# Three transformer blocks on one core: score maps on paired half rows, heads one chunk apart, and a first norm whose scale comes from token rows

## The chip, the cores and the metric

The kernel runs on one core of one Trainium2 chip. The metric is the device time of one execution in microseconds, the median over the runs. TensorE multiplies a stationary operand (a weight load, PEld in the profile) by a moving one into PSUM; VectorE (DVE), ScalarE (ACT) and GpSimd (POOL) do the elementwise work; SP issues nearly all DMAs.

## What is computed

256 tokens of width 1024 go through a first block and two equal blocks of a second kind. The first block, cut to what matters:

```
h = rms_norm(x, norm_g); proj = h @ w_in          # 1024 x 6144
dq, dk, dv, dg, mq, mk, mv, mg, gates = split(proj)
# differential attention: 4 heads, each with two score maps of 64-wide q and k
s = causal(q[:, m] @ k[:, m].T / 8)  for m in 0, 1
w = softmax(s0) - lam * softmax(s1);  o_a = rms_norm(w @ v) * silu(dg)
# block attention: 8 heads of 64; with 256 tokens there is one block, so it is causal attention
o_b = softmax(causal(q @ k.T / 8)) @ v * silu(mg)
merged = sigmoid(g_a) * (o_a @ w_branch_diff) + sigmoid(g_b) * (o_b @ w_branch_moba)
x = x + merged @ w_out;  x = x + sigmoid(x @ w_ple_gate) * (p @ w_ple)
x = rms_norm(x, final_g)
```

Each later block (twice) normalizes, projects, runs 4 retention heads and 8 stick-breaking heads (`z = q k^T`, strictly causal, log terms summed from the right), merges them with gates, and adds a squared-relu MLP of width 4096. A last norm ends it.

## The kernel before

**Arithmetic.** Every product is made in three matmuls of a reduced 32-bit type. An operand is split into a high part (a copy by ScalarE, which rounds) and a low part (the difference, by VectorE); then high x high, high x low and low x high are added in PSUM. `hilo` (lines 126 to 128) does it for activations, `split` (282 to 287) for weights, `norm_hilo` (194 to 197) for x times the norm's gain. The norm's scale per token is not in that operand: it is applied when a projection is taken out of PSUM.

**Chunks.** The weights come as 189 chunks of 1 MB in one stream. `fetch` (276) loads a chunk into one of three `raw` buffers, `split` makes `wh` and `wl` (three buffers each). The loop at line 1018 does for each chunk i: split chunk i+2, fetch chunk i+5, the matmuls of chunk i with their evacuation (`ch.banks`), and then one step of each thread that was there before. A chunk for `chunk_t` (353) holds 8 k tiles by 256 columns and makes two transposed 128-column tiles; a pair of chunks for `chunk_n` (366) holds k tiles 0 to 3 and 4 to 7 of 512 columns and makes both token halves with tokens on partitions. PSUM has 8 banks: 5 `acc` for the chunks and 3 `aux` for everything else.

**Order.** The program's text gives each engine an order, and a planner that simulates the engines rearranges it by readiness. Instructions stamped with the same order token keep their order among themselves on their engine. All loads but that of the gains are issued by SP in the planned order; a load that needs a free buffer holds those behind it.

**The head.** 14 warm-up matmuls (line 416) run on constants. x comes transposed, in two loads of four k tiles; the gains come through ScalarE's queue (137). Chunk 0 is loaded in two pieces and split in four, one per k tile; chunk 1 in two pieces, split in two. Squares of the x tiles (205, 207) are summed over the k tiles; `norm_scale` (235) sums over partitions by matmuls (220, 223), and gives the scale both as a row for all partitions and as a column for each token half. It runs when the first chunk pair is done, ahead of its evacuation.

**The first block's heads.** `block1_branch` (554) makes q, k and v of a branch in six chunks, then two gate chunks follow for each branch; the order is branch 0, all four gate chunks, branch 1. q and k are scaled and turned by `qk1_turn` (440) into `m1`, two 64-wide halves on 128 partitions. `soft_head` (470) is a thread for one pair of maps. In one step it makes both score maps (131 to 133, operands of 64 rows, `M` in the profile), adds the causal mask by a matmul of the mask with an identity (`mask`, 463), takes the row maxima (487), the exps (488) and the scaling by the reciprocals (494 to 499); in the next step it transposes the weights (505); then it multiplies by v (517, 536). Heads 0 and 1 step one chunk ahead of heads 2 and 3.

**The stick-breaking heads.** `sb_head` (755) makes the scores, adds its mask in the same way (761), and takes abs, exp and ln on ScalarE; a step later come the sums (772, 773), a step later the product with v.

## Time and profile before

| | |
|---|---|
| Median of 3 runs | 1169.01 us (1168.88 to 1169.1) |
| Profiled execution | 1168.73 us |
| Its span, first to last instruction | 1167.0 us |
| Mean granted TensorE clock | 0.997 |
| TensorE busy | 1155.9 us, 99% |
| VectorE, ScalarE, GpSimd busy | 876.3, 707.4, 221.2 us |

A row of the profile names the line, the engine, the operation, out<-in by tile names, partitions x elements and the number of instructions; then busy time, the mean of one, and idle time before it with what ended it. A matmul's busy time reaches to its modelled end, so two matmuls in a row overlap in it; their rate is seen from start to start.

### The profile page before, as it was taken

The page shows a single profiled execution, that of the slowest core. Times are in us where ns is not written, and L with a number is a line of the kernel's source. Part 1 is how long each engine was busy: PE and PEld are TensorE (multiplying, and loading weights), DVE is VectorE, ACT ScalarE, POOL GpSimd, SP SyncE. Part 2 cuts the span into 40 slices and gives each one's busy share as a digit, 9 for nine tenths or more (in the row PEclk, how much of TensorE's full clock was granted, in tenths as well). Part 3 has the DMA queues.
Part 4 walks back from the last instruction along what each step waited for, and adds up shares of the span by engine and source line. Part 5 has one row for each costly group of instructions (what it writes and reads, how often), then busy time and mean ns, then how long its engine had stood idle before and what let it go on. Part 6 is the DMA issues. An engine that isn't in the chain of part 4 may idle for free.

```text
span 1167.0 us, 17530 instructions
## 1 busy us (share of the span) xinstructions
PE 1155.9 (99%) x6642; PEld 1013.0 (87%) x6642; DVE 876.3 (75%) x1433; ACT 707.4 (61%) x1275; POOL 221.2 (19%) x242
## 2 busy tenths in 40 slices
PE   8999999999999999999999999999999999999997
PEld 6888889998888888888888888888888888888887
DVE  7766867778997766678877778987776677967664
ACT  6657656566567776556744646556777555846442
POOL 1014104015641122211000002652112112000001
PEclk9999999999999999999999999999999999999999
DMA  8544435545555444546555556454444555555541
GB/s 312 182 144 145 145 117 181 182 180 196 193 181 179 145 164 163 183 165 220 190 181 185 199 183 213 173 196 178 145 168 157 181 183 196 184 184 211 180 180 37
DMA packets 32164, 206.58 MB, mean 177 GB/s; under 512 B 3920, under 2 KB 6224, under 8 KB 8144
## 3 DMA queue, kind: packets, MB, share of 16 engines
q1 hardware_dynamic: 31936, 205.44, 49.3%
q8 instruction: 52, 0.85, 0.3%
q14 instruction: 32, 0.26, 0.1%
q10 hardware_dynamic: 144, 0.03, 0.0%
HBM read 202.31 MB, written 1.05 MB: 174 GB/s over the span
## 4 chain that ended last, share of the span: by engine, by line
PE 94%; DVE 4%; ACT 1%; issue 1%; DMA 0%; POOLq 0%; POOL 0%; DVEq 0%
PE acc L300 41%; PE acc L303 21%; PE acc L343 20%; DVE wl L287 2%; PE aux L131 2%; PE aux L133 2%; PE aux L132 2%; PE acc L133 1%; PE acc L132 1%; PE acc L131 1%; DVE X L666 1%; PE aux L466 1%; PE aux L773 1%; DVE X L197 1%; PE acc L331 1%
## 5 line engine op out<-in xcount | busy, mean ns | idle before, releaser
L287 DVE TENSOR_TENSOR wl<-raw,wh 128x1024 fp32r<-128x1024 f32 (+1 forms) x380 | 462.8, 1249 | 135.1 <-ACT wh L286 130.4
L286 ACT ACTIVATE wh<-raw 128x1024 fp32r<-128x1024 f32 (+1 forms) x380 | 380.4, 1047 | 198.7 <-PE acc L300 109.0
L300 PE MATMUL acc<-X,wh 128*128 128x512 f32 x1472 | 383.1, 394 | 0.6 <-DVE X L666 0.4
L300 PEld LDWEIGHTS acc<-X,wh 128*128 128x128 f32 x1472 | 263.5, 189 | 47.9 <-issue 1.2
L303 PE MATMUL acc<-X,wl 128*128 128x256 f32 x1472 | 221.5, 283 | 0.0
L303 PEld LDWEIGHTS acc<-X,wl 128*128 128x128 f32 x1472 | 206.8, 190 | 13.6
L320 ACT ACTIVATE f<-acc 128x256 f32<-128x256 f32 x216 | 79.4, 374 | 61.8 <-PE acc L303 61.6
L343 PE MATMUL acc<-wh,X 128*128 128x512 f32 x432 | 111.8, 392 | 0.5 <-DVE f L321 0.5
L321 DVE TENSOR_TENSOR f<-f,acc 128x256 f32<-128x256 f32 x216 | 87.7, 414 | 24.0 <-ACT f L320 22.1
L343 PEld LDWEIGHTS acc<-wh,X 128*128 128x128 f32 x432 | 80.0, 188 | 16.6 <-DVE f L321 0.7
L207 POOL TENSOR_TENSOR sq<-sq,f 128x256 f32<-128x256 f32 x30 | 31.5, 1051 | 274.7 <-ACT f L205 274.3
L666 DVE TENSOR_TENSOR X<-X,acc 128x256 f32<-128x256 f32 x112 | 45.8, 416 | 34.2 <-PE acc L303 33.6
L597 POOL TENSOR_TENSOR sig<-f,nr 128x256 f32<-128x256 f32 x48 | 40.9, 859 | 147.1 <-DVE f L321 122.0
L300 PE MATMUL acc<-A,wh 128*128 128x512 f32 x256 | 64.5, 393 | 0.0
L300 PE MATMUL acc<-B,wh 128*128 128x512 f32 x256 | 64.4, 392 | 0.0
L343 PE MATMUL acc<-wl,X 128*128 128x512 f32 x216 | 60.0, 393 | 0.0
L300 PEld LDWEIGHTS acc<-B,wh 128*128 128x128 f32 x256 | 46.1, 189 | 8.2
L300 PE MATMUL acc<-M,wh 128*128 128x512 f32 x192 | 53.0, 394 | 0.0
L300 PEld LDWEIGHTS acc<-A,wh 128*128 128x128 f32 x256 | 46.0, 189 | 8.1
L343 PEld LDWEIGHTS acc<-wl,X 128*128 128x128 f32 x216 | 40.0, 188 | 7.8
L300 PEld LDWEIGHTS acc<-M,wh 128*128 128x128 f32 x192 | 35.0, 188 | 6.9
L303 PEld LDWEIGHTS acc<-A,wl 128*128 128x128 f32 x256 | 35.1, 190 | 2.5
(224 smaller groups left out, 1687.0 us busy)
## 6 DMA issues: line engine op xcount, KB each, us to landing
raw<-in_wstream_dram SPq DMA_DIRECT2D x187, 1024.0 KB, 4.8
raw<-in_wstream_dram SPq DMA_DIRECT2D x4, 512.0 KB, 7.8
sig<-f SPq DMA_DIRECT2D x32, 64.0 KB, 4.6
B<-in_tables_dram SPq DMA_DIRECT2D x2, 768.0 KB, 6.0
X<-in_xt_dram SPq DMA_DIRECT2D x2, 512.0 KB, 6.3
out_dram<-M SPq DMA_DIRECT2D x4, 256.0 KB, 2.2
M<-in_g_final_dram SPq DMA_DIRECT2D x1, 512.0 KB, 4.5
cst<-in_tables_dram SPq DMA_DIRECT2D x1, 352.0 KB, 10.2
```

Of the source, the lines that this page charges most:

```text
L131: T.matmul(o, lhsT=lh, rhs=rh, start=start, stop=False, skip_group_check=True)
L132: T.matmul(o, lhsT=lh, rhs=rl, start=False, stop=False, skip_group_check=True)
L133: T.matmul(o, lhsT=ll, rhs=rh, start=False, stop=stop, skip_group_check=True)
L286: A.activation(ch.wh[:, k], ch.raw[:, k], AF.Copy)
L287: V.tensor_sub(ch.wl[:, k], ch.raw[:, k], f32(ch.wh[:, k]))
L300: T.matmul(ps, lhsT=ch.wh[:, k, w], rhs=x.rearrange("p c t -> p (c t)"), start=i == 0, stop=False, skip_group_check=True)
L303: T.matmul(ps[:, 0:S], lhsT=ch.wl[:, k, w], rhs=x[:, 0], start=False, stop=i == len(ks) - 1, skip_group_check=True)
L320: A.activation(t, ps[:, S:2 * S], AF.Copy)
L321: V.tensor_add(t, t, ps[:, 0:S])
L343: T.matmul(p[:, 0:w], lhsT=xs[:, k, t], rhs=ws[:, i, o], start=n == 0 and k == 0, stop=n == 2 and k == KT - 1, skip_group_check=True)
L597: G.tensor_mul(store[(c, i)][0][:, k % 2], fold(ps), st.n.rb)
L666: V.tensor_add(X[:, k], X[:, k], ps[:, o:o + S])
```

## The change

* **Head, k tile by k tile.** The gains lie in front of x in one tensor and come with its first tile. The loads of x and of chunk 0 alternate (one tile, one piece, one tile, one piece, two tiles, ...). Chunk 1 is split in four too, and multiplied in the order of chunk 0 (`mm_k`: by k tile, both token halves). Order tokens make ScalarE and VectorE take x tile, weight tile, x tile, and so on. Nine warm-up matmuls instead of 14.
* **First norm.** x comes once more with tokens on partitions (`xn`, 1 MB, issued behind chunk 2). ScalarE squares each row half with a sum; the scale per token is a column at once (`head_r`, at high priority). The row for all partitions, which the transposed gates need, is made three chunks later by four matmuls of ones with a scaled identity (`head_rows`).
* **Maps.** The 12 matmuls of a head alternate between the two maps, that is, between partitions 0 to 63 and 64 to 127; one map is in an `aux` bank, the other in an `acc` bank. An order token strings them together with the last matmul of each of the first 20 chunks. The mask is added by VectorE while it takes the maximum (one instruction, which writes the negated sum to SBUF); the exp then works in place. Scaling by the reciprocals is done by ScalarE.
* **Heads one chunk apart**, with one more chunk between the exps and the transposes, and for the differential heads between the sub-norm and its transpose; four buffers for exps instead of two. The gate chunks of a branch follow that branch. Both maps of a block-attention head are multiplied by v together (512 and 256 moving columns).
* **Stick-breaking heads.** The mask is added by VectorE. The buffers `ph` and `pl` hold two sets each, two of them instead of four single ones, for retention and norms too.

The diff, cut to its core (`mm` stands for `T.matmul` in the chunk loops):

```diff
-WARM = 14
+WARM = 9
+GW = 64
+PB = 2
...
+LAST1 = 20
...
+    def mm(*args, **kw):
+        last[0] = T.matmul(*args, **kw)
...
-    gc = tl([56], "gc")
-    nc.scalar.dma_start(out=gc, in_=a["gains"])
+    xg = tl([GW + KT * S], "X")
+    gc, X = xg[:, 0:GW], xg[:, GW:].rearrange("p (k t) -> p k t", k=KT)
+
+    def load_x(k0, k1):
+        sl = slice(GW + k0 * S if k0 else 0, GW + k1 * S)
+        load(xg[:, sl], a["xt"][:, sl])
...
-    msk = tl([384], "sig", bufs=4)
+    msk = tl([384], "msk")
+    tri_f = tl([P], "sig", bufs=4)
...
-    idr = tl([P], "idr", F32R)
-    mqr = tl([P], "mqr", F32R)
-    msr = tl([P], "msr", F32R)
+    m_seg = msk[:, P:2 * P], msk[:, 0:2 * P]
+    m_sb = msk[:, None, 2 * P:3 * P].to_broadcast([P, 2, P])
...
-    def new_norm(g, sub=None):
...
     def fetch(ch, n=1):
+
         ch.raw = shaped(ch, tl([2048], "raw", bufs=3))
         src = shaped(ch, a["wstream"][chunks.index(ch)])
         for k in pieces(ch, n):
             load(ch.raw[:, k], src[:, k])
+            yield
 
     def split(ch, n=2):
+
         ch.wh = shaped(ch, tl([2048], "wh", F32R, bufs=3))
         ch.wl = shaped(ch, tl([2048], "wl", F32R, bufs=3))
         for k in pieces(ch, n):
-            A.activation(ch.wh[:, k], ch.raw[:, k], AF.Copy)
-            V.tensor_sub(ch.wl[:, k], ch.raw[:, k], f32(ch.wh[:, k]))
+            h = A.activation(ch.wh[:, k], ch.raw[:, k], AF.Copy)
+            l = V.tensor_sub(ch.wl[:, k], ch.raw[:, k], f32(ch.wh[:, k]))
+            yield h, l
...
+            if ch is chunks[1]:
+                mm_k(ch, ps, x(), 4)
             for h in range(2):
-                mm_n(ch, ps[h], x(), 4, h)
+                if ch is not chunks[1]:
+                    mm_n(ch, ps[h], x(), 4, h)
                 run_pre()
                 evac(ps[h] if parts > 1 else ps[h][0], h)
...
-    X = tl([KT, S], "X")
-    n0 = new_norm(g_norm)
+    n0 = new_norm(g_norm, sq=False)
+    xn = tl([2, D], "M2")
     st.n = n0
     x_ = lambda: st.n.x
 
...
-    def head_hilo(i):
-        for k in range(4 * i, 4 * i + 4):
-            norm_hilo(n0, X[:, k], k)
...
-    def head_squares():
-        for k in range(KT):
-            norm_square(n0, X, k)
...
-    e_slot = [scr[:, i * 768:(i + 1) * 768].rearrange("p (m q) -> p m q", m=2) for i in range(2)]
-    o_slot = [scr[:, 1536 + i * 256:1536 + (i + 1) * 256].rearrange("p (h e) -> p h e", h=2) for i in range(2)]
-
-    def start1():
-        norm_scale(n0)
-        rq = tl([2], "rq")
-        V.tensor_scalar_mul(rq, n0.r[:, S:S + 4:2], 0.125)
-        n0.rq = [rq[:, h:h + 1] for h in range(2)]
-
-    pre.append(start1)
+    e_slot = [scr[:, i * 768:(i + 1) * 768].rearrange("p (m q) -> p m q", m=2) for i in range(4)]
+    o_slot = [scr[:, 3072 + i * 256:3072 + (i + 1) * 256].rearrange("p (h e) -> p h e", h=2) for i in range(2)]
+
+    def head_r():
+
+        ss, r, rq = tl([2], "hss"), tl([2], "hr"), tl([2], "rq")
+        for h in range(2):
+            A.activation(xn[:, h], xn[:, h], AF.Square, accum_out=ss[:, h:h + 1])
+        V.tensor_scalar(ss, ss, 1.0 / D, EPS, ALU.mult, ALU.add)
+        rsqrt(r, ss)
+        V.tensor_scalar_mul(rq, r, 0.125)
+        n0.rc, n0.rq = ([t[:, h:h + 1] for h in range(2)] for t in (r, rq))
+
+    def head_rows():
+
+        for _ in range(3):
+            yield
+        ps = aux()[:, 0:S]
+        for h in range(2):
+            dh, dl = tl([P], "ph", F32R, PB), tl([P], "pl", F32R, PB)
+            A.activation(dh, ident, AF.Copy, scale=n0.rc[h])
+            V.scalar_tensor_tensor(dl, ident, n0.rc[h], f32(dh), ALU.mult, ALU.subtract)
+            for d in (dh, dl):
+                T.matmul(ps[:, h * P:(h + 1) * P], lhsT=one_r, rhs=d, start=h == 0 and d is dh, stop=d is dl,
+                         skip_group_check=True)
+        n0.rb = tl([W], "nr")[:, 0:S]
+        V.tensor_copy(n0.rb, ps)
+        yield
+
+    threads.append(head_rows())
...
-    m1 = Pair("M2")
...
-    def mask(ps, m):
-
-        o = ps.rearrange("p (b s) -> p b s", b=2)[:, :, 0:P]
-        T.matmul(o, lhsT=idr, rhs=m[:, None, :].to_broadcast([P, 2, P]), start=False, stop=True, skip_group_check=True)
...
-        ps = [aux(), aux()]
-        for m in range(2):
-            r = slice(m * 64, m * 64 + 64)
-            for o, q0, kn in ((0, 0, 128), (128, 128, 256)):
-                q, k = slice(q0, q0 + 128), slice(0, kn)
-                mm3(ps[m][:, o:o + kn], qh[r, q], ql[r, q], kh[r, k], kl[r, k], o == 0, False)
-            mask(ps[m], mqr)
-        e = e_slot[idx % 2]
+        ps = [aux(), acc()]
+        for o, q0, kn in ((0, 0, 128), (128, 128, 256)):
+            for n, (q_, k_) in enumerate(((qh, kh), (qh, kl), (ql, kh))):
+                for m in range(2):
+                    r = slice(m * 64, m * 64 + 64)
+                    mm = T.matmul(ps[m][:, o:o + kn], lhsT=q_[r, q0:q0 + 128], rhs=k_[r, 0:kn],
+                                  start=o == 0 and n == 0, stop=n == 2, skip_group_check=True)
+                    tc.stamp_issue_order_token(mm.ins, "maps")
+        e = e_slot[idx % 4]
...
-                V.tensor_reduce(mx[:, i:i + 1], ps[m][:, lo:hi], AX.X, ALU.max, negate=True)
-                act(e[:, m, lo:hi], ps[m][:, lo:hi], AF.Exp, bias=mx[:, i:i + 1], accum_out=sm[:, i:i + 1])
+                em = e[:, m, lo:hi]
+                V.tensor_tensor_reduce(em, ps[m][:, lo:hi], m_seg[h], -1.0, 3e38, ALU.add, ALU.min, mx[:, i:i + 1])
+                act(em, em, AF.Exp, scale=-1.0, bias=mx[:, i:i + 1], accum_out=sm[:, i:i + 1])
...
-                V.tensor_scalar_mul(e[:, 1, lo:hi], e[:, 1, lo:hi], rs[:, 2 + h:3 + h])
+                A.activation(e[:, 1, lo:hi], e[:, 1, lo:hi], AF.Copy, scale=rs[:, 2 + h:3 + h])
                 V.scalar_tensor_tensor(e[:, 0, lo:hi], e[:, 0, lo:hi], rs[:, h:h + 1], e[:, 1, lo:hi], ALU.mult, ALU.add)
         else:
             for m in range(2):
                 for h, lo, hi in segs:
-                    V.tensor_scalar_mul(e[:, m, lo:hi], e[:, m, lo:hi], rs[:, 2 * m + h:2 * m + h + 1])
-        yield
-        wt = []
+                    A.activation(e[:, m, lo:hi], e[:, m, lo:hi], AF.Copy, scale=rs[:, 2 * m + h:2 * m + h + 1])
+        yield
+        yield
+        wh, wl = tl([2, 384], "ph", F32R, 2), tl([2, 384], "pl", F32R, 2)
         for m in range(1 if diff else 2):
             pt = aux()
             for o, _, _ in BLK:
                 T.transpose(pt[:, o:o + P], e[:, m, o:o + P], ident)
-            h, l = tl([384], "ph", F32R, 4), tl([384], "pl", F32R, 4)
-            hilo(h, l, pt[:, 0:384])
-            wt.append((h, l))
+            hilo(wh[:, m], wl[:, m], pt[:, 0:384])
         yield
...
             yield
+            yield
             pt = aux()[:, 0:S]
             for h in range(2):
                 T.transpose(pt[:, h * P:(h + 1) * P], o[:, h], ident)
             V.scalar_tensor_tensor(f, pt, subg, g1[:, idx], ALU.mult, ALU.mult)
...
-            for m in range(2):
-                h, l = wt[m]
-                vc = slice(j * P, (j + 1) * P)
-                mm3(po[:, m], vh[:, 0, vc], vl[:, 0, vc], h[:, 0:256], l[:, 0:256], m == 0, False)
-                mm3(po[:, m, 128:256], vh[:, 1, vc], vl[:, 1, vc], h[:, 256:384], l[:, 256:384], False, True)
+            vc = slice(j * P, (j + 1) * P)
+            mm3(po, vh[:, 0, vc], vl[:, 0, vc], wh[:, :, 0:256], wl[:, :, 0:256], True, False)
+            mm3(po[:, :, 128:256], vh[:, 1, vc], vl[:, 1, vc], wh[:, :, 256:384], wl[:, :, 256:384], False, True)
...
-                        threads.append(soft_head(4 * br + j, j, v, br == 0, 1 + j // 2))
+                        threads.append(soft_head(4 * br + j, j, v, br == 0, 1 + j))
...
-    block1_branch(0)
-    for c, b in enumerate((6, 7, 14, 15)):
-        gate1(c, b)
-    block1_branch(1)
+    for br, gates in ((0, (6, 7)), (1, (14, 15))):
+        block1_branch(br)
+        for c, b in enumerate(gates):
+            gate1(2 * br + c, b)
...
-        dh, dl = tl([384], "ph", F32R, 4), tl([384], "pl", F32R, 4)
+        dh, dl = tl([384], "ph", F32R, 2), tl([384], "pl", F32R, 2)
...
-        mm3(z[:, 256:384], kh[:, j, 128:256], kl[:, j, 128:256], qh[:, j, 128:256], ql[:, j, 128:256], False, False)
-        mask(z, msr)
+        mm3(z[:, 256:384], kh[:, j, 128:256], kl[:, j, 128:256], qh[:, j, 128:256], ql[:, j, 128:256], False, True)
+        zd = z.rearrange("p (b s) -> p b s", b=2)[:, :, 0:P]
+        V.tensor_add(zd, zd, m_sb)
...
-        h_, l_ = tl([384], "ph", F32R, 4), tl([384], "pl", F32R, 4)
+        h2, l2 = tl([2, 384], "ph", F32R, 2), tl([2, 384], "pl", F32R, 2)
+        h_, l_ = h2[:, 0], l2[:, 0]
         hilo(h_, l_, t)
...
-        h_, l_ = tl([384], "ph", F32R, 4), tl([384], "pl", F32R, 4)
+        h_, l_ = h2[:, 1], l2[:, 1]
         hilo(h_, l_, t)
...
+    def in_order(pair):
+        for ins, tok in zip(pair, ("head_act", "head_dve")):
+            tc.stamp_issue_order_token(ins.ins, tok)
...
     warm_up(WARM)
-    load_x(0)
-    fetch(chunks[0], 2)
-    load_x(1)
-    fetch(chunks[1], 2)
-    fetch(chunks[2])
-    head_hilo(0)
-    split(chunks[0], 4)
-    head_hilo(1)
-    split(chunks[1])
-    fetch(chunks[3])
-    head_squares()
+    f = fetch(chunks[0], 4)
+    load_x(0, 1)
+    next(f)
+    load_x(1, 2)
+    next(f)
+    load_x(2, 4)
+    drain(f)
+    load_x(4, 6)
+    f = fetch(chunks[1], 2)
+    next(f)
+    load_x(6, KT)
+    drain(f)
+    drain(fetch(chunks[2]))
+    load(xn, a["xn"])
+    for i in range(2):
+        f = split(chunks[i], 4)
+        for k in range(4 * i, 4 * i + 4):
+            in_order(norm_hilo(n0, X[:, k], k))
+            in_order(next(f))
+        drain(f)
+    drain(fetch(chunks[3]))
+    with tc.high_priority():
+        head_r()
+    m1 = Pair("M2")
     late_consts()
-    fetch(chunks[4])
+    drain(fetch(chunks[4]))
     for i, ch in enumerate(chunks):
         if i + 2 < n:
-            split(chunks[i + 2])
+            drain(split(chunks[i + 2]))
         if i + 5 < n:
-            fetch(chunks[i + 5])
+            drain(fetch(chunks[i + 5]))
         ready = list(threads)
         ch.banks(ch)
+        if i < LAST1:
+            tc.stamp_issue_order_token(last[0].ins, "maps")
         if i == 0:
             use_consts()
         for g in ready:
```

More of the change, by code (lines that the diff above doesn't have):

```diff
@@ L33 @@
 C_SB = 704
-C_MQ = 704
-C_MS = 832
-C_TRI = 960
-C_DEC = 1088
+C_Z = 704
+C_MQ = 832
+C_MS = 960
+C_TRI = 1088
+C_DEC = 1216
 C_ALL = C_DEC + 4 * 384
 NCHUNK = 189
+LAST1 = 20
 def _tables():
@@ L128, in hilo @@
         V.tensor_sub(lo, src, f32(hi))
+    last = [None]
+    def mm(*args, **kw):
+        last[0] = T.matmul(*args, **kw)
     def mm3(o, lh, ll, rh, rl, start, stop):
@@ L170, in use_consts @@
         V.tensor_scalar_mul(subg, subg, 1.0 - LAM_INIT)
-        V.tensor_copy(idr, ident)
-        V.tensor_copy(mqr, msk[:, 0:128])
-        V.tensor_copy(msr, msk[:, 128:256])
-        V.tensor_copy(tri, msk[:, 256:384])
+        V.tensor_copy(tri, tri_f)
         V.tensor_scalar_mul(neg1, ones, -1.0)
@@ L184, in tile_blocks, with new_norm @@
         pass
-    def new_norm(g, sub=None):
+    def new_norm(g, sub=None, sq=True):
         n = Norm()
@@ L189, in new_norm @@
         n.x = Pair("X2")
-        n.sq = tl([S], "sq")
+        n.sq = tl([S], "sq") if sq else None
         n.sq2 = tl([S], "M2") if sub is not None else None
@@ L194, in norm_hilo @@
     def norm_hilo(n, x, k):
-        A.activation(n.x.h[:, k], x, AF.Copy, scale=n.g[:, k:k + 1])
-        V.scalar_tensor_tensor(n.x.l[:, k], x, n.g[:, k:k + 1], f32(n.x.h[:, k]), ALU.mult, ALU.subtract)
+        h = A.activation(n.x.h[:, k], x, AF.Copy, scale=n.g[:, k:k + 1])
+        l = V.scalar_tensor_tensor(n.x.l[:, k], x, n.g[:, k:k + 1], f32(n.x.h[:, k]), ALU.mult, ALU.subtract)
+        return h, l
     def norm_square(n, X, k):
@@ L330, in mm_k @@
                 for n, (xs, ws) in enumerate(((x.h, ch.wh), (x.h, ch.wl), (x.l, ch.wh))):
-                    T.matmul(ps[h][0], lhsT=xs[:, k, t], rhs=ws[:, i], start=n == 0 and k == 0,
-                             stop=n == 2 and k == KT - 1, skip_group_check=True)
+                    mm(ps[h][0], lhsT=xs[:, k, t], rhs=ws[:, i], start=n == 0 and k == 0,
+                       stop=n == 2 and k == KT - 1, skip_group_check=True)
     def mm_n(ch, ps, x, k0, h):
@@ L342, in mm_n @@
                     k = k0 + i
-                    T.matmul(p[:, 0:w], lhsT=xs[:, k, t], rhs=ws[:, i, o], start=n == 0 and k == 0,
-                             stop=n == 2 and k == KT - 1, skip_group_check=True)
+                    mm(p[:, 0:w], lhsT=xs[:, k, t], rhs=ws[:, i, o], start=n == 0 and k == 0,
+                       stop=n == 2 and k == KT - 1, skip_group_check=True)
     pre = []
```

27 lines of the change are left out of this document (14 added, 13 removed).

## Prediction

> **What bounds the kernel now.** I read the page first: the share of each engine and the chain that ended last.
>
> ```profile
> span 1167.0 us, 17530 instructions
> PE 1155.9 (99%) x6642; PEld 1013.0 (87%) x6642; DVE 876.3 (75%) x1433; ACT 707.4 (61%) x1275; POOL 221.2 (19%) x242
> PE 94%; DVE 4%; ACT 1%; issue 1%; DMA 0%; POOLq 0%; POOL 0%; DVEq 0%
> ```
>
> TensorE is busy for 99% of the span and carries 94% of the chain. So a nanosecond taken out of its instruction stream is a nanosecond off the end, as long as the other engines keep up, and work moved to other engines costs nothing until one of them is late. Next I asked for the waits of PE, which tell where it stands still.
>
> ```profile
> PE acc L331 <- ACT wh L286: 2.2, 1, 2.2
> PE aux L416 <- DVE one_r L152: 1.3, 1, 1.3
> PE acc L343 <- DVE f L321: 0.5, 1, 0.5
> ```
>
> Only the start has a wait worth naming; nothing can be won from stalls later on. The busy time of a matmul is modelled to its end, so cost is read from start to start. The chain of waits, asked for a stretch of the last stage, gives the unit:
>
> ```profile
> 1028.38 21.79 PE acc L343 x96
> 1050.16 1.81 PE acc L300 x8
> 1051.98 0.95 PE acc L303 x8
> ```
>
> A matmul with 512 moving columns takes 21.79 / 96 = 0.227 us of the stream, one with 256 columns 0.95 / 8 = 0.119. Last, the busy time by stretch where the first block's heads run, since the change gives work there to other engines (us, then busy time and instructions of each engine):
>
> ```profile
> 42.00:82.00 40.00, 40.00 (x229) 33.07 (x228) 28.51 (x55) 22.89 (x49) 2.99 (x4) 1.00 0.40 137
> 82.00:120.00 38.00, 37.50 (x193) 31.39 (x192) 26.17 (x55) 29.11 (x71) 13.47 (x16) 1.00 0.40 143
> 120.00:170.00 50.00, 49.95 (x320) 43.55 (x319) 36.63 (x78) 32.11 (x73) 5.89 (x8) 1.00 0.34 125
> ```
>
> In these 128 us VectorE (third number) works 91.3 us, ScalarE (fourth) 84.1: 71% and 66%.
>
> **Part 1, the head.** The timeline of the first 17 us:
>
> ```profile
> 1.30 5.55 PE L416 MATMUL aux<-one_r 128*128 128x512 f32 x14 [1.30 <-DVE one_r L152]
> 5.56 0.42 ACT L205 ACTIVATE sq<-X 128x256 f32<-128x256 f32 x1 [3.12 <-DMA X<-in_xt_dram]
> 6.50 1.69 ACT L196 ACTIVATE X<-X,gc 128x256 fp32r<-128x256 f32 x4
> 7.02 2.62 DVE L197 SCALAR_TENSOR_TENSOR X<-X,gc,X 128x256 fp32r<-128x256 f32 x4 [1.06 <-ACT X L196]
> 8.40 2.17 ACT L286 ACTIVATE wh<-raw 128x512 fp32r<-128x512 f32 x4
> 9.07 1.11 PE L331 MATMUL acc<-wh,X 128*128 128x512 f32 x2 [2.22 <-ACT wh L286]
> 9.57 2.49 DVE L287 TENSOR_TENSOR wl<-raw,wh 128x512 fp32r<-128x512 f32 x4
> 11.75 1.27 PE L331 MATMUL acc<-wh,X 128*128 128x512 f32 x3
> 16.30 0.39 PE L331 MATMUL acc<-wh,X 128*128 128x512 f32 x1
> ```
>
> The matmul at 16.30 is the 24th and last of chunk 0. At 0.227 us each the 23 before it would need 5.2 us, so the stream stands as if it had run densely from 16.30 - 5.2 = 11.1 us. The real start is at 9.07: the first weight split waits behind squares and all four x tiles on ScalarE, the next matmuls wait for VectorE, and three of them run about 0.42 us apart (1.27 / 3), half speed, after a pause of 2.2 us.
>
> With the change one k tile of x (with the gains, 160 KB) and one of the weights (256 KB) come first, and the order on both engines is x tile, weight tile, x tile. The traffic of today's first 10 us, in slices of 0.25 us, and its transfers:
>
> ```profile
> GB/s 0 0 0 0 0 0 49 115 267 204 258 135 174 240 242 176 226 275 236 285 234 229 295 246 311 377 442 361 459 410 410 459 377 442 410 410 459 393 410 377
> X<-in_xt_dram SPq DMA_DIRECT2D x2, 512.0 KB, 6.3
> gc<-in_gains_dram ACTq DMA_DIRECT2D x1, 28.0 KB, 5.0
> ```
>
> Bytes flow from 1.6 us, at some 220 GB/s until 6 us and 410 after. 416 KB take 1.9 us at 220, so they are there no earlier than 3.5 us, and no later than the 5.5 us at which today's 512 KB of x release ScalarE; I take the middle, 4.5. Then come one x tile (1.69 / 4 = 0.42) and one weight tile (2.17 / 4 = 0.54) on ScalarE: the first matmul at about 5.5, just behind nine warm-up matmuls (1.30 + 9 x 5.55 / 14 = 4.9). Per k tile VectorE then needs 2.62 / 4 + 2.49 / 4 = 1.28 us and PE 6 x 0.227 = 1.36, so PE sets the pace. I add 0.8 us for about four first matmuls at half clock: dense from 6.3, 11.1 - 6.3 = **4.8 us** gained. Bounds: 6.1 (dense from 5.0) and 2.0 (x as late as today, 7.0, six slow matmuls, 0.8 us of late tiles: dense from 9.1). Supply behind it: through chunk 2 and the 1 MB of token rows 5.3 million bytes are to be moved, at 410 GB/s by about 15 us, chunk 3 2.6 us later, and chunk 3 is due at 6.3 + 3 x 5.45 = 22.6. The token rows pass SP's queue ahead of chunk 3; the wait of chunk 3 for a free raw buffer ends earlier too, because chunk 0 is split earlier. The norm's sums on PE (six short matmuls) go and four matmuls for the row of scales come: taken as nothing, covered by no wait.
>
> **Part 2, the score maps.** PE's timeline of the second map of head 0, with the mask of the first before it:
>
> ```profile
> 51.58 0.39 PE L466 MATMUL aux<-mqr,idr 128*128 128x256 f32 x1
> 51.89 0.32 PE L131 MATMUL aux<-M 64*128 64x128 f32 x1
> 52.06 0.27 PE L132 MATMUL aux<-M 64*128 64x128 f32 x1
> 52.16 0.27 PE L133 MATMUL aux<-M 64*128 64x128 f32 x1
> 52.28 0.33 PE L131 MATMUL aux<-M 64*128 64x256 f32 x1
> 52.45 0.28 PE L132 MATMUL aux<-M 64*128 64x256 f32 x1
> 52.56 0.27 PE L133 MATMUL aux<-M 64*128 64x256 f32 x1
> 52.77 0.39 PE L466 MATMUL aux<-mqr,idr 128*128 128x256 f32 x1
> 52.99 0.86 PE L300 MATMUL acc<-X,wh 128*128 128x512 f32 x3
> ```
>
> Six half-row matmuls take 52.77 - 51.89 = 0.88 us, a mask 0.31 when half rows follow (51.58 to 51.89) and 0.22 otherwise: turning from 128 to 64 rows costs 0.09, and back also (52.56 to 52.77 is 0.21, the one before 0.11). A head is 2 x 0.88 + 0.31 + 0.22 = 2.29 us. In the new form there are 12 half-row matmuls with no mask and one turn back, 0.09. No row shows two half-row matmuls on different row halves side by side, so I bound them. Without any overlap each takes what one of its kind takes in a run, 0.11 to 0.12 (52.06 to 52.16, 52.45 to 52.56): 12 x 0.115 + 0.09 = 1.47, 0.82 saved. With full overlap two cost what one does, 0.057 each: 0.78, 1.51 saved. If every alternation cost the turn of 0.09: 2.55, 0.26 lost. The matmul rows lean to neither of the first two, so I take their middle, 0.086 each: 1.12, 1.17 saved, for 8 heads **9.3 us** (bounds -2.1 and 12.1).
> The Trainium skill, "TensorE: Matmul & The Clock Gate", part 3 on packing small matmuls, says that matmuls on different row groups run at once, a few ns apart; by it the part is 12.1 instead of 9.3. No row here tests that. Its page "TensorEngine Tiling (Array Packing)", key properties, says a switch of tiling mode drains the array; the 0.31 against 0.22 above agrees, and it would put no such price on alternating row halves.
>
> **Part 3, the other masks.** In the later layers' 16 stick-breaking heads:
>
> ```profile
> 363.13 0.33 PE L466 MATMUL aux<-msr,idr 128*128 128x256 f32 x1
> 363.30 0.28 PE L131 MATMUL aux<-M 128*128 128x256 f32 x1
> ```
>
> 0.17 each, **2.7 us** saved. In its place VectorE adds 128x256 from PSUM, 0.41 us by the same shape at line 321, in front of the head's ScalarE chain. What hides it is the next chunk's 32 matmuls (5.5 us) between a head's scores and the sums that use them; gone, it costs 16 x 0.41 = 6.6.
>
> **Part 4, weights times values of the block-attention heads.** One map of one head now:
>
> ```profile
> 159.29 0.33 PE L131 MATMUL aux<-ph,vh 128*128 128x256 f32 x1
> ...
> 159.70 0.22 PE L131 MATMUL aux<-ph,vh 128*128 128x128 f32 x1
> ...
> 159.98 0.52 PE L505 MATMUL aux<-cst,B 128*128 128x128 f32 x3
> ```
>
> 0.69 us, 1.38 for both. Joined: three matmuls of 512 and three of 256 columns, 3 x 0.227 + 3 x 0.119 = 1.04. Four heads: **1.4 us** (bounds 0.8 and 1.6).
>
> **Part 5, what the other engines get.** Scaling by the reciprocals moves to ScalarE: 4 x 2 + 4 x 4 = 24 copies. The gates of the second branch now lie among its heads, so by program order sigmoid and exp alternate more: some four table loads more.
>
> ```profile
> L525 ACT ACTIVATE B<-aux,ss 128x128 f32<-128x128 f32 x8 | 2.5, 366 | 0.3 <-POOL ss L523 0.3
> L112 ACT ACT_TABLE_LOAD x3 | 3.8, 1283 | 0.1
> ```
>
> 24 x 0.37 + 4 x 1.28 = 14 us more on ScalarE: 98 us of work in about 117, 84%. Queued behind a late exp are the weight splits (two chunks ahead, 11 us of cover) and the folds that free PSUM banks. VectorE gets lighter. The extra chunk between a head's exps and its transposes, and heads one chunk apart instead of two at a time, cover the longer chain. I set **1.0 us** of new stalls against the sum (bounds 0 and 6).
>
> **Sum.** 4.8 + 9.3 + 2.7 + 1.4 - 1.0 = 17.2. The profiled execution took 1168.7 us around a span of 1167.0, 0.3 below the median of the runs, 1169.0: 1168.7 - 17.2 = 1151.5, against the median 1151.8.
>
> **The rivals.**
> *No overlap of half rows.* Weight loads are recorded one after the other, and a pair may cost two. For it: each half-row matmul today starts no sooner than 0.11 after the last. Against it: those share rows. 0.82 x 8 = 6.6 instead of 9.3: 1154.5.
> *Full overlap*, the skill's rule: 1149.0.
> *Alternation is dear*, 0.09 at each change of half, as at a change of row count: part 2 turns into -2.1, 1163.2.
> *The head gives little.* The squares of the token rows stand in ScalarE's queue ahead of chunk 2's split; ScalarE works in order, so they hold the splits until the 1 MB has landed near 16 us, and PE, due at 17, waits for 2 to 3 us. For it: squares at 5.56 ran ahead of everything today. Against: chunk 2 lands first. Head 2.0: 1154.6.
> *The scores hold a PSUM bank of the projections.* Slower: each head now takes one of five accumulators. A bank comes round after five further uses, about 2.8 us each in the gate chunks, so some 11 us after the scores; if VectorE and ScalarE read them later than that, PE stops. From 14 us on, 8 heads x 3 us = 24 are lost: 1176. Against it: VectorE has a quarter of its time free, and today's heads come in twos and PE does not wait for them.
>
> **How the numbers follow.** Forecast as summed 0.42 (its own range 1149 to 1155), no overlap 0.20, full overlap 0.15, small head 0.12, dear alternation 0.07, held bank 0.04. Cutting the dearest cases leaves 1146 (full overlap and the best head) to 1160. A change within 0.2% (2.3 us) is what a measurement of this kernel cannot tell from none. Only the held bank reaches it or passes it; other cases would need several mishaps. Faster 0.92, same 0.04, slower 0.04.
>
> **What would show it.** Head: first weight matmul near 5.5 us and the 24th of chunk 0 near 11.5. Maps: 12 half-row matmuls within 1.1 us, and pairs starting less than 0.11 us apart if they overlap. No mask matmuls; stick-breaking scores followed at once by other work. PE's waits still below 3 us in all, ScalarE near 84% between 35 and 155 us. I am wrong if the half rows need over 1.5 us a head, if PE waits for exps or banks, or if chunk 2 waits for its split.

## The result and the profile after

| | before | after |
|---|---|---|
| Median | 1169.05 us (1168.88 to 1169.45, 4 runs) | 1152.44 us (1151.95 to 1152.50, 4 runs) |
| Profiled execution | 1168.73 us | 1152.48 us |
| Its span | 1167.0 us | 1150.5 us |

The ratio after to before is 0.9856, interval 0.9844 to 0.9868: faster by 16.6 us, or 1.4%; the forecast was 17.2 (1151.8). The page of the kernel after, its totals and the shares of the chain that ended last:

```profile
span 1150.5 us, 17428 instructions
PE 1139.5 (99%) x6579; PEld 998.6 (87%) x6579; DVE 874.3 (76%) x1457; ACT 717.7 (62%) x1302; POOL 221.6 (19%) x236
PE 91%; DVE 4%; DMA 2%; ACT 2%; issue 1%; POOL 0%; SPq 0%; POOLq 0%; DVEq 0%
```

TensorE's busy time fell by 16.4 us and the span by 16.5. TensorE still sets the end. New in the chain is DMA with 2%: the start now hangs on transfers. The waits of PE in the kernel after (us in total, times, longest):

```profile
PE aux L428 <- DVE one_r L167: 1.3, 1, 1.3
PE aux L484 <- ACT sig L585: 1.1, 1, 1.1
PE aux L501 <- DVE ft L562: 0.8, 1, 0.8
PE acc L137 <- ACT wh L302: 0.5, 1, 0.5
```

The first was there before. The other three stand at places where PE did not wait before; each is followed below. First the head, PE's timeline of the kernel after (start, duration, count, idle time before):

```profile
1.30 4.21 PE L428 MATMUL aux<-one_r 128*128 128x512 f32 x9 [1.30 <-DVE one_r L167]
5.58 1.22 PE L137 MATMUL acc<-wh,X 128*128 128x512 f32 x2
...
11.73 0.39 PE L137 MATMUL acc<-wh,X 128*128 128x512 f32 x1
12.61 0.73 PE L137 MATMUL acc<-wh,X 128*128 128x512 f32 x2 [0.49 <-ACT wh L302]
```

The first weight matmul starts at 5.58 instead of 9.07, and the 24th of chunk 0 at 11.73 instead of 16.30, 4.57 earlier. Then PE waits for chunk 1's weights. A head's maps in the same view:

```profile
50.94 0.32 PE L501 MATMUL aux<-M 64*128 64x128 f32 x1
50.94 0.32 PE L501 MATMUL acc<-M 64*128 64x128 f32 x1
51.10 0.27 PE L501 MATMUL aux<-M 64*128 64x128 f32 x1
51.10 0.27 PE L501 MATMUL acc<-M 64*128 64x128 f32 x1
...
51.82 0.50 PE L137 MATMUL acc<-X,wh 128*128 128x512 f32 x1
```

The two matmuls of a pair start together (over all heads the finer start times lie 2 to 6 ns apart, mostly 3 or 4), and pairs follow each other after 0.11 to 0.17 us, as single ones did before. Twelve take 51.82 - 50.94 = 0.88 us, which is what six took before.

**Where the time came from.** I added, for both traces, each PE instruction's time to the next one's start, by kind, which gives the share of the stream that each kind takes, stalls in front of it included.

| | before | after | gain |
|---|---|---|---|
| Lead at the first matmul of chunk 2 (start, slow clock, first waits) | 21.97 | 18.46 | 3.5 |
| Maps of the 8 heads | 14.53 | 7.41 | 7.1 |
| Their masks | 4.12 | 0 | 4.1 |
| Stick-breaking masks | 2.73 | 0 | 2.7, of which 2.3 reach the end |
| Weights times values, block attention | 5.61 | 4.49 | 1.1 |
| Norm | 0.59 | 0.48 | 0.1 |
| Stall of 0.65 before 88.0 us, gone | 0.65 | 0 | 0.65 |
| New stalls, at 23.9 and at 123.9 us | 0 | 1.25 + 0.99 | -2.2 |

Together 3.5 + 7.1 + 4.1 + 2.3 + 1.1 + 0.1 + 0.65 - 2.2 = 16.7, against 16.5 between the spans. After the first block PE was 14.3 us ahead, at the end 16.7. The difference, 2.4, is close to the 2.3 that the 16 stick-breaking masks cost when they are put back (below). The joined weights-times-values products and the norm are read from the traces alone: no run undoes them, nor the new order of splits in the head.

### The profile page after: what moved, and what is told of

The parts are those of the page before. It is cut to its first block, busy times and chain, and to the rows that moved or that the text cites. A ratio compares the mean times of both kernels' runs of the same rounds, so it can differ in the third digit from the quotient of the medians.

```text
span 1150.5 us, 17428 instructions
## 1 busy us (share of the span) xinstructions
PE 1139.5 (99%) x6579; PEld 998.6 (87%) x6579; DVE 874.3 (76%) x1457; ACT 717.7 (62%) x1302; POOL 221.6 (19%) x236
## 4 chain that ended last, share of the span: by engine, by line
PE 91%; DVE 4%; DMA 2%; ACT 2%; issue 1%; POOL 0%; SPq 0%; POOLq 0%; DVEq 0%
PE acc L137 80%; DVE wl L303 2%; PE acc L142 1%; PE acc L141 1%; PE acc L140 1%; PE aux L142 1%; PE aux L141 1%; PE aux L140 1%; DMA M<-in_xn_dram 1%; DVE X L688 1%; PE aux L797 1%; PE aux L501 1%; ACT wh L302 0%; POOL sig L838 0%; DMA X<-in_xt_dram 0%
## 5 line engine op out<-in xcount | busy, mean ns | idle before, releaser
L137 PE MATMUL acc<-wh,X 128*128 128x512 f32 x448 | 118.8, 394 | 0.6 <-ACT wh L302 0.5
L137 PEld LDWEIGHTS acc<-wh,X 128*128 128x128 f32 x448 | 83.3, 189 | 18.4 <-ACT wh L302 1.9
L220 POOL TENSOR_TENSOR sq<-sq,f 128x256 f32<-128x256 f32 x24 | 27.6, 1150 | 263.9 <-ACT f L218 263.7
L619 POOL TENSOR_TENSOR sig<-f,nr 128x256 f32<-128x256 f32 x48 | 44.7, 940 | 120.1 <-DVE f L338 85.8
L137 PE MATMUL acc<-wl,X 128*128 128x512 f32 x224 | 64.4, 395 | 0.0
L568 POOL TENSOR_TENSOR G<-f,nr 128x256 f32<-128x256 f32 x24 | 22.7, 946 | 84.3 <-DVE f L338 83.9
```

The lines of the kernel that those rows point to most:

```text
L137: last[0] = T.matmul(*args, **kw)
L220: (V if k == KT - 1 else G).tensor_add(sq, sq, t)
L568: G.tensor_mul(dst()[:, k], fold(ps), st.n.rb)
L619: G.tensor_mul(store[(c, i)][0][:, k % 2], fold(ps), st.n.rb)
```

## The experiments

Each experiment starts from the kernel after (1152.44 us) unless it says otherwise. The kernel before took 1169.3 to 1169.4 beside them. Over a whole run TensorE's clock was granted at 0.996 to 1.0 in the mean. In three of the profiles it stood at 0.50 for some microseconds within the first block; that is told where it matters.

**Was it the alternation of the maps?** One map after the other, still without a mask:

```diff
-        for o, q0, kn in ((0, 0, 128), (128, 128, 256)):
-            for n, (q_, k_) in enumerate(((qh, kh), (qh, kl), (ql, kh))):
-                for m in range(2):
-                    r = slice(m * 64, m * 64 + 64)
+        for m in range(2):
+            r = slice(m * 64, m * 64 + 64)
+            for o, q0, kn in ((0, 0, 128), (128, 128, 256)):
+                for n, (q_, k_) in enumerate(((qh, kh), (qh, kl), (ql, kh))):
```

> The changed kernel with one edit: a head's 12 half-row matmuls run map after map (six on partitions 0 to 63, then six on 64 to 127), still without masks and in the same banks. Theory: the pairs overlap fully (3 ns apart in the changed kernel's trace), so a head's 0.78 us become 12 x 0.115 plus about 0.2 of turns, 1.5 us; 8 heads cost 6 us, 1158.4. Rival: alternating is not what matters, the masks and the fewer turns are, and the maps' place in the stream gave the rest: within 1 us of 1152.4.

Measured: 1156.97 us (1156.36 to 1157.70), 4.5 above the kernel after. PE's timeline of this kernel at head 0 and at the last head:

```profile
44.41 0.55 PE L501 MATMUL aux<-M 64*128 64x128 f32 x3
44.70 0.32 PE L501 MATMUL acc<-M 64*128 64x128 f32 x1
44.80 0.33 PE L501 MATMUL aux<-M 64*128 64x256 f32 x1
...
44.97 0.28 PE L501 MATMUL aux<-M 64*128 64x256 f32 x1
...
45.09 0.28 PE L501 MATMUL aux<-M 64*128 64x256 f32 x1
...
128.11 0.52 PE L501 MATMUL aux<-M 64*128 64x128 f32 x3 [1.64 <-DVE ft L562]
...
129.25 1.63 PE L137 MATMUL acc<-X,wh 128*128 128x512 f32 x4
```

The six of `aux` stand ahead of the six of `acc` in the instruction stream: the edit writes them so, and the order token keeps them so. Yet the first of `acc`, at 44.70, starts before the last three of `aux`, at 44.80, 44.97 and 45.09. So the second map runs beside the first without being interleaved by the program, and the maps take 9.28 us in all, 1.9 more than alternated and 5.3 less than before. The time and the total alone would have said "full overlap is worth 4.5 us here"; the trace says 1.9. The rest is at the last head. Two waits, 0.81 and 1.64, stand there instead of one of 0.78, 1.7 us more. Behind them four matmuls take 1.63 us, where four take 1.07 at full rate (the kernel after at 23.00 us, shown below). The view by stretches gives the reason; the third number from the end is TensorE's granted clock:

```profile
130.00:133.00 3.00, 3.00 (x10) 2.41 (x9) 2.60 (x10) 3.00 (x12) 1.41 (x2) 0.50 0.88 309
```

The clock is granted at 0.50 from 129.8 to 133.2 us, which costs about 3.4 x 0.5 = 1.7 us. Together 1.9 + 1.7 + 1.7 = 5.3, against 5.2 between the two profiled executions (1157.70 and 1152.48). Neither of my two theories had this; the first one's 1158.4 lies near for another reason.

**What separated the maps before, then?** The same edit, and the mask between the maps by a matmul as before:

```diff
+            mo = ps[m].rearrange("p (b s) -> p b s", b=2)[:, :, 0:P]
+            mm = T.matmul(mo, lhsT=idr, rhs=mqr[:, None, :].to_broadcast([P, 2, P]), start=False, stop=True,
+                          skip_group_check=True)
+            tc.stamp_issue_order_token(mm.ins, "maps")
```

> The changed kernel with the maps made as before it: map after map, each closed by a mask matmul on TensorE (the mask is added again by VectorE, which changes nothing). In the first run of this study, maps one after the other but without masks took 9.3 us of the stream for 8 heads, against 7.4 paired and 18.7 before, because TensorE began the second map's matmuls before the first's had started: it overlaps row halves even when they are issued apart. Theory: the 128-row mask between the maps is what kept them apart; with it back the maps take 18 to 19 us again, 11 us more than in the changed kernel, 1163 to 1165. Rival: the maps overlap whatever stands between them and only the masks' own 4 us come back: 1156 to 1158.

Measured: 1162.20 us (1161.29 to 1163.30). PE's timeline of this kernel, one head:

```profile
43.41 0.95 PE L504 MATMUL aux<-M 64*128 64x128 f32 x6
44.30 0.39 PE L508 MATMUL aux<-mqr,idr 128*128 128x256 f32 x1
44.61 0.95 PE L504 MATMUL acc<-M 64*128 64x128 f32 x6
45.49 0.39 PE L508 MATMUL acc<-mqr,idr 128*128 128x256 f32 x1
45.72 0.62 PE L137 MATMUL acc<-X,wh 128*128 128x512 f32 x2
```

The halves are apart again: 0.89 and 0.88 for the maps, 0.31 and 0.23 for the masks, 14.09 + 4.29 = 18.4 us for eight heads, as in the kernel before (18.65). Against the maps one after the other without masks that is 9.1 us, of which 4.3 are the masks themselves and 4.8 the overlap that they forbid. One matmul on 128 rows between the two groups is enough. The time rose by 9.8, the stream's maps by 11.0; where 1 us of it came back I did not find.

**The other mask.** The 16 stick-breaking masks by matmul again:

```diff
-        V.tensor_add(zd, zd, m_sb)
+        T.matmul(zd, lhsT=idr, rhs=msr[:, None, :].to_broadcast([P, 2, P]), start=False, stop=True, skip_group_check=True)
```

> The changed kernel with the mask of the stick-breaking heads back on TensorE (16 matmuls of a mask with an identity in place of 16 adds on VectorE). Theory: each mask matmul is 0.17 us of the stream and the add on VectorE is hidden: 2.7 us more, 1155.1. Rival: the add has put 0.4 us in front of each head's chain and PE waits for part of it, so the mask on TensorE costs less than 1.5 us net: below 1153.9.

Measured: 1154.73 us (1154.47 to 1155.48), 2.3 more; the masks take 2.73 us of PE's stream. The sum of the prediction stands, a little smaller, and VectorE's addition is hidden.

**The head.** First, 14 warm-up matmuls as before instead of nine:

```diff
-WARM = 9
+WARM = 14
```

> The changed kernel with 14 warm-up matmuls instead of 9. Theory: the first weight tile is ready at 5.58 us and 14 warm-up matmuls end near 7, so the chunks start 1 to 1.4 us later but at full clock; the two first k tiles catch up little, and the end is 0.5 to 1.2 us later, 1152.9 to 1153.6. Rival: chunk 1 waits for its weights anyway (0.65 us at 12 us) and the transposes for the norm's scale at 24 us, so the later start is hidden: within 0.3 us of 1152.4.

Measured: 1151.94 us (1151.82 to 1152.06), 0.5 less. PE's timeline of this kernel:

```profile
6.48 0.62 PE L137 MATMUL acc<-wh,X 128*128 128x512 f32 x2
...
11.77 0.87 PE L137 MATMUL acc<-wh,X 128*128 128x512 f32 x3
```

Starting 0.9 us later costs nothing at chunk 0: its 24th matmul starts at 11.77, against 11.73. So the head start is not spent on arithmetic alone, it runs ahead of the supply. The stream then runs through into chunk 1 at 11.99, where the kernel after stood until 12.61, but this is not shown to be the warm-up's doing. The first half of chunk 1 landed at 11.2 us in this execution and at 11.9 in the kernel after's, and it moves between 11.2 and 12.3 in the runs with the same loads. The run with the stick-breaking masks has nine warm-up matmuls and is just as far ahead from chunk 3 on (0.56 us; here 0.53). The 0.5 us are therefore within what the landings move; the result lies outside both theories, nearer to the second.

Second, the loads in halves as in the kernel before; the splits and their order stay as changed:

```diff
-    f = fetch(chunks[0], 4)
-    load_x(0, 1)
-    next(f)
...
+    load_x(0, 4)
+    drain(fetch(chunks[0], 2))
+    load_x(4, KT)
+    drain(fetch(chunks[1], 2))
```

> The changed kernel with x and the first two chunks loaded in halves again (x tiles 0 to 3 with the gains, two halves of chunk 0, x tiles 4 to 7, two halves of chunk 1), everything else as changed, the order by k tile on ScalarE and VectorE too. Theory: the small loads give an early first matmul (5.6 us) but move the bytes of chunk 1 later (it landed at 11.9 and 13.8 us, against 11.2 and 12.5 before the change), and chunk 2 starts at the same time with halves, 18.4 us: within 0.5 us of 1152.4; the gain of the head comes from the order of the splits and from the gains in x's load. Rival: the k-tile loads carry it, the first matmul comes at 7.5 us or later and the end 1.0 to 2.0 us later, over 1153.4.

Measured: 1153.17 us (1152.63 to 1154.21), 0.7 more. PE's timeline of this kernel:

```profile
7.33 0.73 PE L137 MATMUL acc<-wh,X 128*128 128x512 f32 x2 [1.82 <-ACT wh L302]
...
10.09 0.63 PE L137 MATMUL acc<-wl,X 128*128 128x512 f32 x1
10.51 0.63 PE L137 MATMUL acc<-wh,X 128*128 128x512 f32 x1
```

The first matmul comes 1.75 us later and, after the pause of 1.82, matmuls follow each other after 10.51 - 10.09 = 0.42 us instead of 0.23. Here too the clock was halved, from 8.9 to 12.3 us:

```profile
9.00:12.00 3.00, 3.00 (x9) 2.35 (x8) 3.00 (x7) 2.93 (x8) 0.00 (x0) 0.50 1.03 427
```

Chunk 2 starts 1.75 us later (20.21 against 18.46), but by chunk 3 only 0.46 is left, because the waits there are shorter. Of the fine loads' 1.75 us, then, 0.7 reach the end by the medians, 0.5 in the profile. The result lies between the two theories.

**The wait at 24 us.** In the kernel after, ScalarE's timeline:

```profile
18.86 1.06 ACT L439 ACTIVATE M<-M 128x1024 f32<-128x1024 f32 x1 [0.53 <-DMA M<-in_xn_dram]
22.95 1.55 ACT L585 ACTIVATE sig<-acc,rq 128x256 f32<-128x256 f32 x4
24.38 2.01 ACT L302 ACTIVATE wh<-raw 128x1024 fp32r<-128x1024 f32 x2
```

and PE's:

```profile
23.00 1.07 PE L137 MATMUL acc<-wh,X 128*128 128x512 f32 x4
25.16 0.63 PE L484 MATMUL aux<-cst,sig 128*128 128x128 f32 x4 [1.09 <-ACT sig L585]
25.54 0.70 PE L137 MATMUL acc<-wh,X 128*128 128x512 f32 x2
```

PE stands before the transposes of the first q, which need the scale from the token rows; chunk 3's split stands behind that evacuation on ScalarE. I moved the transposes one chunk later:

```diff
         def g():
+            if late:
+                yield
             pt = aux().rearrange("p (j t) -> p j t", j=2)
```

> The changed kernel with the transposes of the first branch's q one chunk later. In the changed kernel PE stands still for 1.25 us at 24 us, where these transposes wait for q scaled by the norm's scale, which came from the token rows that landed at 18.8 us. Theory: this wait is a placement and not a bound; with the transposes later it is gone, 1.2 us less, 1151.2. Rival: the chunks that follow would wait in its place (for weights that land near 23 and 26 us, or for PSUM banks that the evacuation frees late), and the time stays within 0.3 us of 1152.4.

Measured: 1152.33 us (1152.21 to 1152.43), no difference. The place in PE's timeline of this kernel:

```profile
25.18 1.19 PE L137 MATMUL acc<-wh,X 128*128 128x512 f32 x4 [0.94 <-ACT wh L302]
```

The wait has moved to chunk 3's weights, 0.94 us, and the transposes follow without one. Both were late. In the DMA issues of the kernel after (KB each, median us to landing) one sees how long the small tables and the token rows were under way:

```profile
M<-in_xn_dram SPq DMA_DIRECT2D x1, 1024.0 KB, 11.4
cst<-in_tables_dram SPq DMA_DIRECT2D x1, 352.0 KB, 11.6
```

Chunk 3 is issued behind the token rows, at 11.98, and lands at 23.0. So I put the token rows behind chunk 3, in the kernel with the later transposes:

```diff
     drain(fetch(chunks[2]))
-    load(xn, a["xn"])
...
-    drain(fetch(chunks[3]))
+    for ins in [next(fetch(chunks[3])), load(xn, a["xn"])]:
+        tc.stamp_issue_order_token(ins.ins, "rows")
```

> The changed kernel with the token rows (1 MB) loaded behind chunk 3 instead of ahead of it, and the first transposes of q one chunk later. Moving the transposes alone changed nothing, because PE then waited for the weight splits of chunk 3, which landed at 23.0 us behind the token rows. Theory: the supply is the bound there; with chunk 3 landing 2.5 us earlier this wait goes as well, 1.0 to 1.5 us less, 1151.2. Rival: the norm's scale then comes 2 to 4 us later, q stays in its PSUM banks until about 27 us, and ScalarE and VectorE, which have to scale q then, split the next chunks late: no gain, within 0.3 us of 1152.4.

Measured: 1150.93 us (1150.78 to 1151.38), 1.5 less. ScalarE's timeline of this kernel:

```profile
20.74 2.01 ACT L301 ACTIVATE wh<-raw 128x1024 fp32r<-128x1024 f32 x2 [2.56 <-DMA raw<-in_wstream_dram]
23.15 1.06 ACT L438 ACTIVATE M<-M 128x1024 f32<-128x1024 f32 x1 [0.40 <-DMA M<-in_xn_dram]
...
28.50 1.55 ACT L588 ACTIVATE sig<-acc,rq 128x256 f32<-128x256 f32 x4
```

Chunk 3's split starts at 20.74 instead of 24.38, the squares go behind it, and the evacuation with its scale waits until 28.5 without harm. Chunk 3's issue hardly moved (11.7 instead of 11.98), its landing did, 20.6 instead of 23.0: what held it up were the bytes of the token rows, not the time of its issue. The supply it was. The token rows later without the later transposes were not run.

**The wait at 124 us.** In the kernel after, PE's timeline and VectorE's:

```profile
124.82 0.29 PE L501 MATMUL aux<-M 64*128 64x128 f32 x1 [0.78 <-DVE ft L562]
```

```profile
123.81 0.86 DVE L562 TENSOR_TENSOR ft<-aux,G 64x256 f32<-64x256 f32 x2 [1.44 <-PE aux L142]
124.70 2.90 DVE L303 TENSOR_TENSOR wl<-raw,wh 128x1024 fp32r<-128x1024 f32 x2
```

The last head's maps need an `aux` bank that the product at line 562 still reads. Three edits touch this place. First, both maps in `acc` banks:

```diff
-        ps = [aux(), acc()]
+        ps = [acc(), acc()]
```

> The changed kernel with both maps of a head in the projections' PSUM banks. In the changed kernel the maps of the last block-attention head wait 1.0 us at 124 us for an aux bank that VectorE is still reading. Theory: this wait goes and none comes, since an acc bank comes round after five uses: 0.8 to 1.0 us less, 1151.5. Rival: two of five acc banks held by a head make the projections wait instead: slower than 1152.4, by 1 us a head if they wait long.

Measured: 1153.67 us (1153.11 to 1153.91), 1.2 more. The wait at 124 is gone, but the maps' share of the stream grows from 7.41 to 8.68. No wait for a bank shows among PE's; in five heads, against two in the kernel after, other matmuls now stand between the twelve, which at the widest are spread over 3.4 us. As far as the trace shows, the cost is in this order, and not in projections that wait for a bank, as the second theory had it. Second, scaling by the reciprocals on VectorE:

```diff
-                A.activation(e[:, 1, lo:hi], e[:, 1, lo:hi], AF.Copy, scale=rs[:, 2 + h:3 + h])
+                V.tensor_scalar_mul(e[:, 1, lo:hi], e[:, 1, lo:hi], rs[:, 2 + h:3 + h])
```

and in the same way for the block-attention heads.

> The changed kernel with the scaling by the reciprocals back on VectorE (24 instructions of 128x128 or 128x256). ScalarE loses the 9.1 us of its lines 518 and 523 in the first block, VectorE gains 6.8. Theory: neither engine's total sets the pace, with two chunks of prefetched weights as cover: within 0.6 us of 1152.4. Rival: ScalarE at 81% in this stretch is what makes the heads' chains late, and the wait for an aux bank at 124 us follows from it: 0.8 us or more faster, under 1151.6.

Measured: 1154.69 us (1153.86 to 1157.42), 2.3 more, which neither theory had. The waits of PE of this kernel, first row, and VectorE's timeline:

```profile
PE aux L501 <- DVE ft L562: 2.3, 1, 2.3
```

```profile
122.66 2.96 DVE L303 TENSOR_TENSOR wl<-raw,wh 128x1024 fp32r<-128x1024 f32 x2
125.54 0.85 DVE L562 TENSOR_TENSOR ft<-aux,G 64x256 f32<-64x256 f32 x2
```

Here the product stands behind a weight split and comes at 125.54 instead of 123.81; the wait grows from 0.8 to 2.3, 1.5 us more. Behind it the granted clock is 0.50 from 126.6 to 133.4 us:

```profile
127.00:133.00 6.00, 6.00 (x26) 5.00 (x25) 5.28 (x22) 4.51 (x14) 1.42 (x2) 0.50 0.42 164
```

That is 6.8 x 0.5 = 3.4 us. Together 1.5 + 3.4 = 4.9, as much as this profiled execution, the slowest of the four (1157.42), lies above the kernel after's. The others took 1153.9 to 1154.9; how much of a slow clock is in them is not on record. Up to 121 us PE is no later than in the kernel after, though the 24 copies are on VectorE. So what costs is the order on VectorE at one place, and the clock that follows the pause, not VectorE's load. Third, heads in twos, as before:

```diff
-                        threads.append(soft_head(4 * br + j, j, v, br == 0, 1 + j))
+                        threads.append(soft_head(4 * br + j, j, v, br == 0, 1 + j // 2))
```

> The changed kernel with the heads stepping two at a time as before (first two one chunk ahead of the last two) instead of one chunk apart. Theory: the longer distance between exps and transposes covers the chain, so spacing is worth little: within 0.6 us of 1152.4. Rival: four exps, reciprocals and copies more at once on ScalarE, at 81% busy, and twice as many banks held at once make PE wait for banks and weights: 2 us or more slower, over 1154.4.

Measured: 1148.96 us (1148.78 to 1149.38), 3.5 less than the kernel after: neither theory had it. With two buffers for their rows, two of the four differential heads write over those of the others before these are transposed, so two outputs of that branch are another head's; the work is of the same amount. With four buffers:

```diff
-    o_slot = [scr[:, 3072 + i * 256:3072 + (i + 1) * 256].rearrange("p (h e) -> p h e", h=2) for i in range(2)]
+    o_slot = [scr[:, 3072 + i * 256:3072 + (i + 1) * 256].rearrange("p (h e) -> p h e", h=2) for i in range(4)]
...
-            o = o_slot[idx % 2]
+            o = o_slot[idx % 4]
```

> The changed kernel with heads stepping two at a time, with four slots for the sub-norm's rows instead of two and the staging tile for the heads' outputs taken only where it is written. In the run with heads in twos and nothing else, the second two differential heads write their rows over those of the first two before these are transposed, so two of four heads' outputs are another head's; its instructions were the same in number and kind, and it took 1149.0. Theory: its 3.5 us come from the order (the wait at 124 us for an aux bank is gone and the last block-attention heads end a chunk earlier), not from the overwriting: 1148.5 to 1149.8. Rival: keeping the rows alive brings waits back: 1151 or more.

Measured: 1148.76 us (1148.31 to 1150.06), 3.7 less, as expected. (The buffer of the product `ft` is also taken only where it is written.) The last head's maps start two chunks earlier, the last of them at 109.4 instead of 125.5 us, and the wait at line 501 is no longer among PE's. That wait is not the whole gain. In the stream the transposes of weights and rows take 3.87 us instead of 5.55, of which 0.95 was the wait, and the maps 6.28 instead of 7.41: two heads' maps now stand next to each other, so the turn between 128 and 64 rows is paid once for both. Last, both gains in one kernel, twos with four buffers and the token rows behind chunk 3:

> Both edits that gained: heads in twos with four row slots, and the token rows behind chunk 3 with the first transposes of q one chunk later. The two gains lie in different stretches (119 to 125 us, and 24 to 27 us). Theory: they add, 3.4 and 1.5 less than 1152.4: 1147.0 to 1148.2. Rival: the later norm scale pushes the first heads' chain into the shorter distance of the twos and part is lost: 1148.8 or more.

Measured: 1148.50 us (1147.45 to 1148.75, 5 runs), ratio to the kernel before 0.9820 (0.9806 to 0.9833). It has the lowest median of all versions, though its range and that of twos with four buffers overlap. Its waits of PE:

```profile
PE aux L427 <- DVE one_r L167: 1.3, 1, 1.3
PE acc L137 <- ACT wh L301: 0.9, 1, 0.9
PE aux L504 <- DVE M L132: 0.4, 1, 0.4
```

The gains hardly add: by the medians 0.3 us more than twos alone, where 1.5 had been measured alone. The result lies between the two theories, and the trace bears out the second. At 36 us this kernel is 1.0 us ahead of the run with twos alone and two buffers, at 48 us 0.2 behind. In between, the first head's maps wait 0.4 us for their operands (the third row above), which the later norm scale delays; the rest of the 1.2 us shows no single wait.

## Why the prediction was right

The forecast was 1151.8, within its own narrow range; measured 1152.44. The signs hold in every part, and the places in all but the new stalls. Sizes differ, and two misses cancel.

* **The head, 4.8.** The first matmul (5.58, forecast 5.5) and the 24th (11.73, forecast 11.5) came as worked out, the second in part by luck: the 0.8 us set down for a half clock did not occur (the granted clock is 1.00 from 4 to 8 us), but 0.9 us went into waits for late pieces instead (11.73 - 5.58 is 6.15, where 23 matmuls need 5.2). But 1.1 of the lead of 4.6 was gone at chunk 2's start (3.5), and another 1.25 at 24 us. The failed step is "supply behind it": chunk 3 was to land about 17.6 us and landed at 23.0. Three things were left out. My own rates, 220 GB/s until 6 us and 410 after, bring 5.3 million bytes by 16.6 us and not by 15. The 608 KB of small tables, issued between 8.09 and 10.62, stood ahead of chunk 3 as well, 1.5 us at 410. And between 6 and 12 us the small pieces moved at 255 to 385 GB/s and not 410, some 1.1 us. That makes about 21.8; the rest stays open. Nor did chunk 3's issue come earlier with its free buffer: chunk 0's last split ends at 10.68 instead of 12.06, but the issue moved only from 12.09 to 11.98. SP's issues there each stand right behind the landing of an earlier load (7.42 behind 7.40, 9.31 behind 9.30, 11.98 behind 11.90). The rival of a small head named the token rows' squares in front of chunk 2's split; it was chunk 3, and the rows' transfer rather than their squares. The runs with the loads in halves and with the token rows later show the supply as the limit; the one with 14 warm-up matmuls agrees.
* **The maps, 9.3.** Measured 11.2, the term that was mis-sized. I took the middle between no overlap and full overlap; it is full overlap. Twelve half-row matmuls take what six did, 0.88 a head and not 1.12, so 2.29 falls to about 0.9. My bound for full overlap, 12.1, was too high: it counted 0.11 for each pair, where my own rows show 0.17 behind the first of each three and 0.88 for six; 8 x (2.29 - 0.88) = 11.3 is what they gave. In the Trainium skill, "TensorE: Matmul & The Clock Gate", part 3, matmuls on distinct row groups run concurrently, with starts about 4 ns apart; the trace agrees (2 to 6 ns, mostly 3 or 4). The same part states that matmuls never start out of program order; the run with one map after the other disagrees, with a start at 44.70 ahead of three earlier-issued ones at 44.80 to 45.09, and the measurement decides. My reason for the middle, "the matmul rows lean to neither", overlooked that the old trace could not show overlap because a 128-row mask stood between the maps; the run with that mask put back shows it to be the barrier.
* **The stick-breaking masks, 2.7.** 2.3 at the end. The cover named (the next chunk's 32 matmuls) held.
* **Weights times values, 1.4.** 1.1, within the bounds.
* **New stalls, 1.0.** 2.2 new against 0.65 gone, 1.6 net. PE's named waits are about 4.5 us, not under 3. The wait at 124 was not foreseen in kind: not a late exp, but a late product that holds an `aux` bank. The rival of the held bank (24 us) did not come in its form; moving both maps to `acc` banks costs 1.2, again without a wait for a bank.
* **ScalarE at 84%.** The windows view of the kernel after, 35 to 155 us:

```profile
35.00:155.00 120.00, 119.12 (x719) 101.60 (x718) 87.29 (x202) 94.49 (x219) 24.35 (x28) 1.00 0.46 162
```

94.49 / 120 = 79%, with the table loads it was charged for:

```profile
L116 ACT ACT_TABLE_LOAD x7 | 9.0, 1283 | 0.1
```

Seven between 30 and 165 us, three before: four more, as forecast. Neither these nor the 24 copies stand among PE's waits.

So the total was right to 0.6 us because maps that gave 1.9 more paid for a head that gave 1.3 less, stalls of 0.6 more and the two small terms (0.7 less). The mechanisms of the large terms were right; that the total came this near is luck. I did not ask what the step of the heads by one chunk costs by itself: part 5 counts it as cover, and heads in twos with enough row buffers are 3.7 us faster.

## What to carry to other kernels

Two matmul groups on different row halves run side by side if nothing of full height stands between them; before pricing such an overlap, look whether the old trace could have shown it. A head start on the bound engine is worth only what the transfers behind it can follow, so list each transfer between the start and the first full buffer, small tables too. When the bound engine stands still, look at the granted clock behind the pause (in two runs here its halving cost as much as the pause or more), and look which instruction is in front of the one it needs: an order or a buffer changed at that place moved 1 to 4 us here, while four table loads and 24 copies more on an engine with room cost nothing that shows.
